# Seven block products in another order: weight sums on VectorE instead of accumulating transfers

## The chip, the cores and the metric

The program runs on one core of a Trainium2 chip. The metric is the device time of one execution in microseconds (us), as the median of several runs. The engines are TensorE (PE for matmuls, PEld for its weight loads), VectorE (DVE), ScalarE (ACT), GpSimd (POOL) and SyncE (SP). SP and POOL each issue transfers from a queue of their own, in order.

## The reference

Two layers of a decoder trunk on x (256 tokens x 2048). Each layer normalises x, projects it by one wide matrix w_in into everything that three token mixers A, B and C need and into the merge gates, runs the mixers, projects each by its own matrix, merges the three by sigmoid gates, and adds a last projection to x. The lines that matter here:

```python
h = rms_norm(x, norm_w)
proj = h @ w_in
...
y_b = (conformer_conv(ub, conv_w, conv_b, cln_w, cln_b) * jax.nn.silu(zb)) @ w_b_out
...
g = jax.nn.sigmoid(gates).reshape(b, s, N_BRANCH, D_MODEL)
merged = g[:, :, 0] * y_a + g[:, :, 1] * y_b + g[:, :, 2] * y_c
return x + merged @ w_out
```

The change touches two products per layer: the last two 512-column chunks of the gates of branch B (columns 1024 to 2047 of `g[:, :, 1]`), and two chunks of `merged @ w_out`.

## The kernel before

**Products in three parts.** Every fp32 operand is split into a high part, which a matmul takes in the fast 32-bit form, and a low rest. A product is the sum of high by high, low activation by high weight, and high activation by low weight. For the weights, ScalarE casts the raw block to `wh` (L246, `high`), and VectorE subtracts, `wl = raw - wh` (L250, `low`). These two are called the cast and the low step below. Matmuls come in the order of that sum, so the low part of the weights is needed last.

**Units.** Work on weights goes by units. An ordinary unit (`plain`) is one 512 KB block of weights, 2 x 128 rows by 512 columns: one transfer on SP's queue into a `raw` buffer (L235, four buffers), one cast, one low step (`wh` and `wl` have three buffers each), and 12 matmuls, 8 with `wh` and 4 with `wl`. `run(units, tasks)` walks a list of units. While it writes out unit n it issues the transfer of unit n+4 (after that unit's `before` functions) and the cast and the low step of unit n+2. After the products come the unit's `now` functions, one entry of `tasks`, and whatever is due of the transposes that go through memory (`zt`, `z`, `zy`).

**Order.** Inside `run` the order of VectorE is the order in which the code is written (`tc.manual_schedule(engines={nc.vector.engine})`). On the other engines a scheduler that estimates times chooses the order, TensorE's too. All queues are in order: what stands behind a waiting instruction waits too.

**Seven products.** `seven` computes a product of 2 x 2 blocks with seven block products in place of eight. It takes the first 1024 of the 2048 rows of weights and two chunks of 512 columns. The blocks of weights are B11, B12, B21, B22 (512 x 512, 1 MB each, in halves h of 512 KB); the blocks of the activations and their differences (`forms`, kept as `sums`) are prepared beforehand. Each block product is two half-units ("subs") of 6 matmuls, 4 with `wh` and 2 with `wl`, so there are 14 subs per call. They are put between ordinary units: every second unit in the w_out stretch, about every third in the gates stretch. Results gather in four PSUM banks X, Y, Z, W; V, U1, U2 and R5 are combinations that are set aside.

**Weights of the subs, before.** Two blocks are held in SBUF slots, "all" (first B11) and "two" (first B22), each fetched by two transfers on SP's queue (`fetch`, L439). The sums are made by transfers that add into the held block (`more`, L454, on POOL's queue): after the cast and the low step of a sub have read it, B12, B22 and B21 are added to "all" in turn and B12 to "two". That makes eight accumulating transfers of 512 KB per call. Only the product by B21 comes as ordinary units.

There are four such stretches, two per layer. They are called G0 and W0 (gates and w_out of the first layer) and G1 and W1 (second layer). The units of a stretch are numbered from 0 (u0, u1, ...). In W0 and W1 subs 0, 1, 2, 3 are units 2, 4, 6, 8, and units 5, 7 and 9 are ordinary; in G0 and G1 subs 0 to 3 are units 2, 4, 7 and 10.

## Time and profile before

| | |
|---|---|
| Median of 3 runs (lowest to highest) | 2014.24 us (2012.94 to 2014.68) |
| Profiled execution, its own time | 2013.33 us, span 2011.6 us |
| PE, PEld, DVE, ACT, POOL busy | 2001.1, 1677.8, 1595.5, 1093.6, 210.1 us |
| Transfers | 463.80 MB, mean 231 GB/s |
| Granted TensorE clock | 0.999 |
| Accumulating transfers L454 | 32 of 512 KB |

In the views below, a group or a timeline row names the line, the engine, the operation and the tiles written and read; `x8` is a count. In the windows view each engine has its busy time in the window and the number of its instructions; after them come the granted clock and the busy share of the transfer engines. The profile puts a matmul's end where the pipeline model has it, so rows overlap; starts are what counts.

### The profile page before, as it was taken

How to read it: one execution, taken by the hardware profiler on the slowest of the kernel's cores; microseconds unless marked ns; L12 is line 12 of the kernel's file. 1: busy time of each engine (PE TensorE's matmuls, PEld its weight loads, DVE VectorE, ACT ScalarE, POOL GpSimd, SP SyncE). 2: the span in 40 equal slices, each digit the busy share in tenths (PEclk: the TensorE clock that was granted, in tenths of full speed). 3: DMA queues.
4: the chain of work that ended last, by engine and by line, in shares of the span. 5: the costliest groups of instructions: out<-in, count | busy, mean ns of one | idle time of the engine just before them, and what ended most of it. 6: DMA issues, size and time to landing. Idle time of an engine off the chain costs nothing.

```text
span 2011.6 us, 25827 instructions
## 1 busy us (share of the span) xinstructions
PE 2001.1 (99%) x9338; PEld 1677.8 (83%) x9338; DVE 1595.5 (79%) x2124; ACT 1093.6 (54%) x1261; POOL 210.1 (10%) x316
## 2 busy tenths in 40 slices
PE   9999999999999999999999999999999999999998
PEld 8889888888888888888888988888888888888876
DVE  8667899878878876677785779988889788756777
ACT  7556555565644555455564555555656445544564
POOL 0111112100010001212210111111000100012120
PEclk9999999999999999999999999999999999999999
DMA  7788678866676678979987886788666766789795
GB/s 267 230 286 263 189 226 287 246 178 179 180 223 193 182 226 236 279 225 298 290 246 233 278 249 188 234 279 249 178 177 177 221 198 190 226 247 267 235 299 169
DMA packets 235585, 463.80 MB, mean 231 GB/s; under 512 B 17280, under 2 KB 30080, under 8 KB 235328
## 3 DMA queue, kind: packets, MB, share of 16 engines
q1 hardware_dynamic: 206592, 385.06, 62.1%
q0 software_dynamic: 27200, 73.94, 13.9%
q10 hardware_dynamic: 1664, 3.15, 0.4%
q8 instruction: 73, 1.20, 0.3%
q14 instruction: 56, 0.46, 0.1%
HBM read 429.31 MB, written 32.77 MB: 230 GB/s over the span
## 4 chain that ended last, share of the span: by engine, by line
PE 97%; DMA 2%; DVE 0%; ACT 0%; issue 0%; POOL 0%; DVEq 0%; ACTq 0%; POOLq 0%
PE acc L260 84%; PE mm L260 10%; DMA raw<-in_w_out_dram 1%; PE mm L1036 1%; DMA z<-zt 1%; PE mm L1126 0%; DMA zy<-z 0%; PE mm L1094 0%; PE mm L1231 0%; PE mm L1177 0%; ACT wh L246 0%; PE mm L795 0%; PE mm L1207 0%; PE mm L1097 0%; PE mm L1006 0%; PE mm L1236 0%
## 5 line engine op out<-in xcount | busy, mean ns | idle before, releaser
L260 PE MATMUL acc<-wh,s 128*128 128x512 f32 (+1 forms) x5088 | 1259.7, 389 | 1.4 <-ACT wh L246 1.0
L246 ACT CAST wh<-raw 128x1024 fp32r<-128x1024 f32 (+1 forms) x698 | 730.8, 1048 | 767.3 <-PE acc L260 510.8
L260 PEld LDWEIGHTS acc<-wh,s 128*128 128x128 f32 x5088 | 946.9, 188 | 190.9 <-ACT wh L246 2.4
L250 DVE TENSOR_TENSOR wl<-raw,wh 128x1024 fp32r<-128x1024 f32 (+1 forms) x699 | 846.4, 1214 | 319.6 <-ACT wh L246 317.1
L260 PE MATMUL acc<-wl,s 128*128 128x512 f32 (+1 forms) x2352 | 626.2, 388 | 0.0
L260 PEld LDWEIGHTS acc<-wl,s 128*128 128x128 f32 x2352 | 440.8, 188 | 90.2 <-DVE wl L250 1.0
L292 POOL DMA_DIRECT2D z<-zt x196 | 117.6, 616 | 1250.2 <-DVE zt L289 907.6
L605 DVE SCALAR_TENSOR_TENSOR s<-yT,cst,s 128x256 f32<-128x256 f32 x480 | 212.2, 478 | 0.0
L260 PE MATMUL mm<-wh,s 128*128 128x512 f32 x480 | 123.6, 389 | 0.1
L260 PEld LDWEIGHTS mm<-wh,s 128*128 128x128 f32 x480 | 90.0, 188 | 19.2 <-ACT wh L246 0.5
L250 DVE TENSOR_TENSOR wl<-s,wh 128x1024 fp32r<-128x1024 f32 x48 | 58.5, 1219 | 18.4 <-ACT wh L246 18.1
L246 ACT CAST wh<-s 128x1024 fp32r<-128x1024 f32 x48 | 50.5, 1053 | 40.8 <-PE acc L260 22.9
L260 PEld LDWEIGHTS mm<-s,wl 128*128 128x128 f32 x512 | 66.9, 191 | 5.0
L260 PE MATMUL mm<-wl,s 128*128 128x512 f32 x240 | 68.8, 390 | 0.0
L260 PE MATMUL mm<-s,wl 128*128 128x192 f32 x512 | 66.0, 271 | 0.0
L298 POOL DMA_DIRECT2D zy<-z x50 | 36.0, 720 | 268.7 <-DMA z<-zt 140.8
L260 PEld LDWEIGHTS mm<-wl,s 128*128 128x128 f32 x240 | 45.0, 188 | 9.7 <-DVE wl L250 0.4
L289 DVE STREAM_TRANSPOSE zt<-acc 128x512 f32<-128x512 f32 (+1 forms) x68 | 45.4, 681 | 8.2 <-PE acc L260 8.2
L454 POOL DMA_DIRECT2D s<-in_w_in_dram x16 | 19.2, 1203 | 115.7 <-DVE wl L250 100.8
L543 DVE TENSOR_TENSOR s<-zy,s 128x1024 fp32r<-128x1024 f32 x20 | 24.3, 1215 | 5.1 <-ACT s L542 5.1
L542 ACT CAST s<-zy 128x1024 fp32r<-128x1024 f32 x20 | 21.0, 1048 | 11.8 <-DVE zy L593 7.0
L1313 DVE TENSOR_TENSOR ev<-acc,ev 128x512 f32<-128x512 f32 x24 | 16.5, 688 | 11.9 <-PE acc L260 11.9
(280 smaller groups left out, 1093.4 us busy)
## 6 DMA issues: line engine op xcount, KB each, us to landing
raw<-in_w_in_dram SPq DMA_DIRECT2D x539, 512.0 KB, 4.5
raw<-in_w_out_dram SPq DMA_DIRECT2D x52, 512.0 KB, 7.2
zy<-z POOLq DMA_DIRECT2D x48, 512.0 KB, 5.2
z<-zt POOLq DMA_DIRECT2D x188, 128.0 KB, 4.6
raw<-in_w_a_dram SPq DMA_DIRECT2D x32, 512.0 KB, 3.9
raw<-in_w_c_dram SPq DMA_DIRECT2D x32, 512.0 KB, 4.4
raw<-in_w_b_dram SPq DMA_DIRECT2D x32, 512.0 KB, 5.0
s<-in_w_in_dram POOLq DMA_DIRECT2D x16, 512.0 KB, 8.3
```

Of the source, the lines that this page charges most:

```text
L246: newest_parts[0] = nc.scalar.copy(u[1], u[0])
L250: newest_parts[1] = sub = nc.vector.tensor_sub(u[2], u[0], u[1].bitcast(F32))
L260: newest[0] = nc.tensor.matmul(o, lhsT, rhs, start=start, stop=stop, skip_group_check=True)
L289: nc.vector.transpose(tmp[:, t].rearrange("p b k i -> p k b i"), src.rearrange("p k (b c) -> p k b c", b=4, c=32))
L292: nc.gpsimd.dma_start(z[:, :, :, a, :].rearrange("t b c e -> c (t b) e"), tmp[a * 32:(a + 1) * 32].rearrange("c t b k i -> c (t b) (k i)"))
L298: nc.gpsimd.dma_start(y.rearrange("p (t a) k i -> p t (a k i)", a=4), z.rearrange("t b c a e -> (b c) t (a e)"))
L454: nc.gpsimd.dma_start(grow[g][:, hs, :], block(add, h), accum_op=ALU.add)
L542: nc.scalar.copy(h, src)
L543: nc.vector.tensor_sub(l, src, h.bitcast(F32))
L605: nc.vector.scalar_tensor_tensor(o, yT[:, c, q:q + S], wq, o, op0=ALU.mult, op1=ALU.add)
L1036: nc.tensor.matmul(ps[:, q * S:(q + 1) * S], qi[i][:, hd, :], ki[j][:, 0, :], start=n == 0, stop=n == 2)
L1313: nc.vector.tensor_mul(sg[t], y[t], sg[t])
```

## The change

The seven products come in another order, with other forms of the activations where they need it, and three of the four block sums are made by VectorE. B11 and B22 are fetched at units 0 and 1 (before: 0 and 8 in the gates, 0 and 5 in w_out). B12 comes as two ordinary units, subs 2 and 3. A new hook `early` runs three units ahead, in front of the low step of the unit two ahead: for subs 2 and 3 it adds B12 to the held B11, and then B22 to the `raw` buffer that holds B12; for subs 6 and 7 it adds B22 to the held sum. Only B21 is still added by a transfer (`by_transfer`), after subs 6 and 7. B21 also comes as ordinary units, subs 10 and 11. U1 now takes two steps on VectorE, one of them after sub 3.

```diff
-        def fetch(g, b):
-            grow[g] = slot().rearrange("p (k a) t -> p k (a t)", a=2)
+        def fetch(b):
+            v = slot().rearrange("p (k a) t -> p k (a t)", a=2)
             with tc.high_priority():
                 for h in range(2):
-                    nc.sync.dma_start(grow[g][:, h * 2:h * 2 + 2, :], block(b, h))
+                    held[b, h] = v[:, h * 2:h * 2 + 2, :]
+                    nc.sync.dma_start(held[b, h], block(b, h))
+
+        def add(h, to, b):
+            nc.vector.tensor_add(held[to, h], held[to, h], held[b, h])
...
-            def more():
-                with tc.high_priority():
-                    nc.gpsimd.dma_start(grow[g][:, hs, :], block(add, h), accum_op=ALU.add)
...
-        subs = [sub(h, *v) for v in (("all", "12", act, 0, 0, X), ("21", None, act, 4, 0, X),
-                                     ("all", "22", sums, 4, 1, Z), ("two", "12", sums, 4, 0, Z),
-                                     ("all", "21", sums, 0, 0, Y), ("two", None, sums, 0, 1, Y),
-                                     ("all", None, act, 4, 1, W)) for h in range(2)]
+        subs = [sub(h, *v) for v in (("11", act, 0, 0, X), ("12", sums, 0, 1, Y), ("11", sums, 4, 1, Z),
+                                     ("11", sums, 0, 0, Y), ("22", sums, 4, 0, Z), ("21", act, 4, 0, X),
+                                     ("11", act, 4, 1, W)) for h in range(2)]
+        for h in range(2):
+            for n, last_use, b in ((2, 0, "12"), (6, 4, "22"), (12, 6, "21")):
+                if b in by_transfer:
+                    subs[last_use + h].more = lambda h=h, b=b: nc.gpsimd.dma_start(held["11", h], block(b, h), accum_op=ALU.add)
+                else:
+                    subs[n + h].early = [partial(add, h, "11", b)]
+            subs[2 + h].early = [*subs[2 + h].early, partial(add, h, "12", "22")]
         subs[1].now = [lambda: nc.scalar.copy(V, X)]
+        subs[3].now = [lambda: nc.vector.tensor_add(U1, V, Y)]
         subs[5].now = [lambda: nc.vector.tensor_sub(R5, Z, V)]
-        subs[9].now = [lambda: nc.vector.tensor_sub(U1, Y, V)]
-        subs[11].now = [lambda: nc.vector.tensor_sub(U2, V, Y)]
+        subs[7].now = [lambda: nc.vector.tensor_sub(U1, Y, U1), lambda: nc.vector.tensor_sub(U2, V, Y)]
...
+            with tc.high_priority():
+                if 0 <= n + 3 < len(units):
+                    for f in units[n + 3].early:
+                        f()
             if 0 <= n + 2 < len(units):
                 high(got[n + 2])
                 low(got[n + 2])
...
-        for n, *b in ((0, "all", "11"), (8, "two", "22")):
+        for n, b in ((0, "11"), (1, "22")):
```

How instructions stand on an engine before and after is shown at three places. In the rows, `raw`, `wh` and `wl` are a unit's buffers, `s8` a slot (a held block or a part of an activation), `long` the activation's differences before their split, `acc` the sums of ordinary units, `mm` two of the banks X, Y, Z, W.

VectorE at the start of W0, before: the split of a merged chunk (L543, from `zy`), the low steps of units 4 and 5, the first half of the split of `sums`, the low steps of units 6 and 7, the second half of that split, and the low steps of units 8 and 9.

```order
L543 TENSOR_TENSOR s8_1360_7776<-zy_1328_7619,s8_1360_7776 128x4x256
L250 TENSOR_TENSOR wl_1353_7729<-s8_1340_7707,wh_1352_7728 128x1024
L250 TENSOR_TENSOR wl_1357_7751<-raw_1355_7748,wh_1356_7750 128x1024
L543 TENSOR_TENSOR s8_1338_7703<-long_1264_7263,s8_1338_7703 128x4x256
L250 TENSOR_TENSOR wl_1363_7782<-raw_1361_7779,wh_1362_7781 128x1024
L250 TENSOR_TENSOR wl_1366_7795<-raw_1364_7792,wh_1365_7794 128x1024
L543 TENSOR_TENSOR s8_1337_7702<-long_1264_7263,s8_1337_7702 128x4x256
L250 TENSOR_TENSOR wl_1369_7815<-raw_1367_7812,wh_1368_7814 128x1024
```

The same place on VectorE after the change (its lines L443 are the adds, L555 is the split).

```order
L555 TENSOR_TENSOR s8_1363_7783<-zy_1330_7624,s8_1363_7783 128x4x256
L250 TENSOR_TENSOR wl_1356_7737<-s8_1342_7712,wh_1355_7736 128x1024
L443 TENSOR_TENSOR s8_1342_7712<-s8_1342_7712,raw_1364_7786 128x1024
L443 TENSOR_TENSOR raw_1364_7786<-raw_1364_7786,s8_1346_7719 128x1024
L250 TENSOR_TENSOR wl_1360_7758<-raw_1358_7755,wh_1359_7757 128x1024
L555 TENSOR_TENSOR s8_1340_7708<-long_1266_7269,s8_1340_7708 128x4x256
L250 TENSOR_TENSOR wl_1366_7789<-raw_1364_7786,wh_1365_7788 128x1024
L443 TENSOR_TENSOR s8_1342_7712<-s8_1342_7712,raw_1370_7820 128x1024
L443 TENSOR_TENSOR raw_1370_7820<-raw_1370_7820,s8_1346_7719 128x1024
L250 TENSOR_TENSOR wl_1369_7801<-raw_1367_7798,wh_1368_7800 128x1024
L555 TENSOR_TENSOR s8_1339_7707<-long_1266_7269,s8_1339_7707 128x4x256
L250 TENSOR_TENSOR wl_1372_7823<-raw_1370_7820,wh_1371_7822 128x1024
```

Two adds now stand in front of unit 5's low step and two more in front of unit 7's, so unit 7's low step is the tenth row where it was the sixth.

TensorE at the same place, before: units 5 to 9, each sub (`mm`) whole between ordinary units (`acc`).

```order
L260 MATMUL acc_1354_7733<-wl_1357_7751,s8_1324_7593 128x512 x4
L260 MATMUL mm_1335_7700<-wh_1362_7781,s8_1324_7593 128x512 x4
L260 MATMUL mm_1335_7700<-wl_1363_7782,s8_1324_7593 128x512 x2
L260 MATMUL acc_1354_7733<-wh_1365_7794,s8_1360_7776 128x512 x8
L260 MATMUL acc_1354_7733<-wl_1366_7795,s8_1360_7776 128x512 x4
L260 MATMUL mm_1335_7700<-wh_1368_7814,s8_1324_7593 128x512 x4
L260 MATMUL mm_1335_7700<-wl_1369_7815,s8_1324_7593 128x512 x2
L260 MATMUL acc_1354_7733<-wh_1373_7832,s8_1360_7776 128x512 x8
```

TensorE after the change; `s8_1339` is the half of `sums` that the last split on VectorE above makes.

```order
L260 MATMUL acc_1357_7740<-wl_1360_7758,s8_1326_7598 128x512 x4
L260 MATMUL mm_1338_7706<-wh_1365_7788,s8_1339_7707 128x512 x2
L260 MATMUL acc_1357_7740<-wh_1368_7800,s8_1363_7783 128x512 x8
L260 MATMUL acc_1357_7740<-wl_1369_7801,s8_1363_7783 128x512 x4
L260 MATMUL acc_1357_7740<-wh_1375_7837,s8_1363_7783 128x512
L260 MATMUL mm_1338_7706<-wh_1365_7788,s8_1339_7707 128x512 x2
L260 MATMUL mm_1338_7706<-wl_1366_7789,s8_1339_7707 128x512 x2
L260 MATMUL mm_1338_7706<-wh_1371_7822,s8_1339_7707 128x512 x4
L260 MATMUL mm_1338_7706<-wl_1372_7823,s8_1339_7707 128x512 x2
L260 MATMUL acc_1357_7740<-wh_1375_7837,s8_1363_7783 128x512 x7
```

Sub 2 now starts with two matmuls, unit 7 is put in between, and the rest of sub 2 stands behind the first matmul of unit 9. W1 has the same piece; nowhere else does TensorE's order of units change.

SP's queue at the start of W1, after the change: the final norm's weights, B11's first half, the last unit of w_b, B22's first half, w_out's units, then the second halves of both.

```order
L1416 DMA s8_2807_15956<-in_fnw_dram 128x2048
L440 DMA s8_2813_15965<-in_w_out_dram 128x2x512
L235 DMA raw_2799_15875<-in_w_b_dram 128x2x512
L440 DMA s8_2817_15972<-in_w_out_dram 128x2x512
L235 DMA raw_2814_15968<-in_w_out_dram 128x2x512
L235 DMA raw_2818_15975<-in_w_out_dram 128x2x512
L235 DMA raw_2823_15983<-in_w_out_dram 128x2x512
L235 DMA raw_2829_16008<-in_w_out_dram 128x2x512
L235 DMA raw_2835_16039<-in_w_out_dram 128x2x512
L235 DMA raw_2838_16051<-in_w_out_dram 128x2x512
L440 DMA s8_2813_15965<-in_w_out_dram 128x2x512
L440 DMA s8_2817_15972<-in_w_out_dram 128x2x512
```

Before, B22's halves stood behind the transfers of units 9 and 17, and B11's second half in front of unit 6's; now B11's second half stands behind unit 7's, and B22's first half in front of unit 0's.

## The prediction

> **What bounds the kernel now.** I read the page first, then windows, then single stretches in order of time.

> ```profile
> span 2011.6 us, 25827 instructions
> PE 2001.1 (99%) x9338; PEld 1677.8 (83%) x9338; DVE 1595.5 (79%) x2124; ACT 1093.6 (54%) x1261; POOL 210.1 (10%) x316
> PE 97%; DMA 2%; DVE 0%; ACT 0%; issue 0%; POOL 0%; DVEq 0%; ACTq 0%; POOLq 0%
> ```

> TensorE is busy for 99% of the span, and the chain that ended last runs through it for 97%. The change leaves the number of matmuls as it is. So what it can win is TensorE's waiting inside the four stretches G0, W0, G1 and W1, and what it can lose is new waiting. The windows view says how much waiting there is.

> ```profile
> core 0: us, PE busy (x) PEld busy (x) DVE busy (x) ACT busy (x) POOL busy (x), PEclk, DMA share, GB/s
> 900.00:950.00 50.00, 49.70 (x219) 40.84 (x218) 40.52 (x43) 29.21 (x32) 12.24 (x15) 1.00 0.98 299
> 1650.00:1700.00 50.00, 50.00 (x223) 41.40 (x222) 43.36 (x47) 24.07 (x25) 0.00 (x0) 1.00 0.63 189
> 1900.00:1950.00 50.00, 49.19 (x216) 40.05 (x215) 38.75 (x41) 27.44 (x30) 12.26 (x15) 1.00 1.01 314
> ```

> The window from 1650 lies outside the change and holds 223 matmuls. The start of W0 (from 900) has 219, the start of W1 (from 1900) 216, and there the transfer engines are full. Matmul starts tell more exactly; this is TensorE in W0, units 5 to 9:

> ```profile
> 931.08 1.07 PE L260 MATMUL acc<-wl,s 128*128 128x512 f32 x4
> 931.99 1.07 PE L260 MATMUL mm<-wh,s 128*128 128x512 f32 x4
> ...
> 936.97 0.61 PE L260 MATMUL mm<-wl,s 128*128 128x512 f32 x2
> 937.89 2.11 PE L260 MATMUL acc<-wh,s 128*128 128x512 f32 x8 [0.30 <-ACT wh L246]
> 939.83 1.07 PE L260 MATMUL acc<-wl,s 128*128 128x512 f32 x4
> 940.74 1.07 PE L260 MATMUL mm<-wh,s 128*128 128x512 f32 x4
> ```

> Four matmuls from 931.08 to 931.99 give 0.227 us per start. Two from 936.97 should end at 937.42, and the next starts at 937.89; the eight from there take 1.94 in place of 1.81. So one wait costs 0.60, of which 0.13 is a slow restart. Unit 9 ends at 940.74. The same in W1:

> ```profile
> 1935.70 0.61 PE L260 MATMUL mm<-wl,s 128*128 128x512 f32 x2
> 1937.05 2.14 PE L260 MATMUL acc<-wh,s 128*128 128x512 f32 x8 [0.74 <-ACT wh L246]
> 1939.03 1.08 PE L260 MATMUL acc<-wl,s 128*128 128x512 f32 x4
> 1939.94 1.07 PE L260 MATMUL mm<-wh,s 128*128 128x512 f32 x4
> 1940.85 0.61 PE L260 MATMUL mm<-wl,s 128*128 128x512 f32 x2
> 1941.54 2.11 PE L260 MATMUL mm<-wh,s 128*128 128x512 f32 x8
> 1943.49 1.08 PE L260 MATMUL mm<-wl,s 128*128 128x512 f32 x4
> ```

> By the same count 1.07 is lost ahead of 1939.03 and 0.38 around 1941.54. At the end of G1 a late transpose costs about 0.4: ScalarE, in order, waits for it and then casts late.

> ```profile
> 1858.20 1.05 ACT L542 CAST s<-zy 128x1024 fp32r<-128x1024 f32 x1 [3.71 <-DMA zy<-z]
> ```

> So 0.60 + 1.07 + 0.38 + 0.4 = 2.45 us is about all that the change can win.

> **Transfers.** Over four calls the accumulating halves fall from 32 to 8, and the ordinary halves grow by 8. That is 16 halves of 0.52 MB fewer, 8.4 of 463.8 MB. POOL's queue loses 24 of its transfers, and the `z` transposes stand behind fewer. What that is worth is read from landing times, in the full stretch 1925 to 1962, around the start of W0 (905 to 945), and in a quiet one, 750 to 790:

> ```profile
> raw<-in_w_out_dram SPq DMA_DIRECT2D x11, 512.0 KB, 10.1
> raw<-in_w_out_dram SPq DMA_DIRECT2D x13, 512.0 KB, 6.5
> raw<-in_w_in_dram SPq DMA_DIRECT2D x11, 512.0 KB, 3.7
> ```

> A block lands 10.1, 6.5 and 3.7 after its issue. I take the wait behind unit 9 in W1 as gone (-0.38; 0 if landings stay as they are) and G1's late transpose too (-0.4; 0 if it comes late for another reason). The 0.60 and 1.07 are replaced by what follows.

> **Adds.** VectorE gets 24 steps of 128x1024, and four half as long for U1. A low step has that size, so its price stands in VectorE's rows of W0:

> ```profile
> 925.18 1.18 DVE L543 TENSOR_TENSOR s<-zy,s 128x1024 fp32r<-128x1024 f32 x1
> 926.28 1.22 DVE L250 TENSOR_TENSOR wl<-s,wh 128x1024 fp32r<-128x1024 f32 x1
> 927.41 1.22 DVE L250 TENSOR_TENSOR wl<-raw,wh 128x1024 fp32r<-128x1024 f32 x1
> 928.55 1.22 DVE L543 TENSOR_TENSOR s<-long,s 128x1024 fp32r<-128x1024 f32 x1
> 929.68 2.36 DVE L250 TENSOR_TENSOR wl<-raw,wh 128x1024 fp32r<-128x1024 f32 x2
> 931.95 1.22 DVE L543 TENSOR_TENSOR s<-long,s 128x1024 fp32r<-128x1024 f32 x1
> 933.09 1.22 DVE L250 TENSOR_TENSOR wl<-raw,wh 128x1024 fp32r<-128x1024 f32 x1
> ```

> One takes 1.22, and the next starts 1.135 after it did. All of them are 24 x 1.22 = 29 us of an engine that is 79% busy, and most fit into its idle time. Here they don't: from 925.18 to 934.3 VectorE has no gap, and four adds go in.

> **W0.** The row at 927.41 is unit 5's low step. Two adds take its place. I count 1.22 around adds, since they use each other's buffers, and 1.135 elsewhere: adds at 927.41 and 928.63, unit 5's low step at 929.85 (done 931.07, and TensorE wants it at 931.08), the split at 930.98, unit 6 at 932.12, adds at 933.25 and 934.47, unit 7's low step at 935.69, done 936.9. TensorE in its new order does two matmuls of sub 2 from 931.99 and eight of unit 7, so it wants that `wl` at 931.99 + 10 x 0.227 = 934.26. It waits 2.65.

> Then it has four matmuls, to 937.8, and the first of unit 9, which needs unit 9's cast. That cast reuses unit 7's `wh` buffer, free at 936.9. Its block goes into the `raw` buffer of unit 5, so its issue follows unit 5's low step, from this row to 931.07:

> ```profile
> 928.66 0.37 SPq L235 DMA_DIRECT2D raw<-in_w_out_dram  x1
> ```

> With the landing of 6.5 it is there at 937.6, cast at 938.6: a wait of 0.8 (0.1 with a landing under 5.8, 2.3 with the 8.0 that this transfer took before, beside transfers of which two are gone). 22 more matmuls to unit 9's end (5.0) and two restarts (0.26): 943.85 in place of 940.74, **+3.1** (+1.5 to +4.5; the low end if the adds follow at 1.135 and VectorE comes to the piece earlier). Behind the adds on VectorE queue the second half of the split of `sums`, which the rest of sub 2 needs, and unit 8's low step. Both are done by 939.2, before TensorE gets there.

> **W1.** The same piece starts at 1924.67, 0.51 earlier on its axis, and unit 9's end at 1939.94, 0.80 earlier. One thing is added: B11's second half stood ahead of the three transfers of this row and now stands behind the second of them, unit 7's. Sub 1's cast needs it.

> ```profile
> 1917.49 5.10 SPq L235 DMA_DIRECT2D raw<-in_w_out_dram  x3
> ```

> ```profile
> 1921.98 1.05 ACT L246 CAST wh<-s 128x1024 fp32r<-128x1024 f32 x1
> 1925.77 1.21 DVE L250 TENSOR_TENSOR wl<-s,wh 128x1024 fp32r<-128x1024 f32 x1
> ```

> Unit 7's goes out one VectorE step after unit 6's, at about 1918.6. Issued at 1919 and landing 6 later, it is cast by 1926.1 in place of 1923.0, and sub 1's low step, at 1925.77 before, comes 0.35 late (0 to +0.9), with all behind it. In W0 unit 7's low step is done 11.72 after the piece's start (936.9 - 925.18); here it is 11.72 + 0.35 after 1924.67, at 1936.75. The rest as in W0 (0.91 + 0.8 + 5.0 + 0.26) ends at 1943.7 in place of 1939.94: +3.8. B22's first half also goes out ahead of unit 0's block, whose cast already waits:

> ```profile
> ACT wh L246 <- DMA raw<-in_w_b_dram: 2.9, 1, 2.9
> ```

> 0.52 MB at the window's 314 GB/s is 1.7 us, part of it covered by slack of unit 0: +0.4 (0 to +1.2). With -0.38 from above, W1: **+3.8** (0 to +5.5).

> **G0 and G1.** The adds for sub 2 come before unit 6's low step. In G0:

> ```profile
> 800.48 3.49 DVE L250 TENSOR_TENSOR wl<-raw,wh 128x1024 fp32r<-128x1024 f32 x3
> 812.76 1.07 PE L260 MATMUL acc<-wl,s 128*128 128x512 f32 x4
> ```

> Unit 6 is the second of these three. It ends at 805.3 in place of 802.8, and only then is its buffer free for sub 3's B12. That lands at 809.0 (3.7) to 815.4 (10.1); two adds (2.4) and unit 9's low step (1.2) follow, 812.6 to 819, and TensorE wants it at 812.76. With the accumulating transfers gone I take a landing near the quiet end and **+0.3** for each (0 to +3 each; I cut the far end, since 10.1 belongs to W1).

> **Sum.** 3.1 + 3.8 + 0.6 - 0.4 = +7.1. The profiled execution took 2013.33 (span 2011.6 and 1.7 around it), so 2020.4. The median of the runs is 0.9 above that execution: 2021.3.

> [...]

> **Rivals.** *Same:* the jam is smaller, because landings fall so far that casts and splits reach VectorE earlier and the adds start ahead of 927.41. For it: the transfer engines are full exactly there. Against it: from 925.18 on each row has a known length, and none ahead of it is removed. With 1.5 in W0, 1.5 - 0.38 in W1, nothing in G0, -0.4 in G1: +2.2, so 2016.4. *Faster:* transfers are the true limit and the adds hide. All of the 2.45 won gives 2011.8, 0.12% and still not over 0.2%; it decides only if TensorE also starts matmuls faster. The 1650 window speaks against that: it fills 50 us with 223 starts at a transfer share of 0.63. *Much slower:* sub 3's B12 lands late in G0 and G1 (the 3 us ends): +5.4 more than the sum, 2026.7. It decides from a landing of 3.9 on, and each further us there costs 2 us in total.

> [...]

> **Chances.** A difference under 0.2%, 4 us, can't be told from none. Jam as computed 0.50, much slower 0.08, same 0.38, faster 0.04. The jam's own spread is about 2018 to 2024, so nearly all of it is slower by over 0.2% (from 2018.3): slower 0.57, same 0.40, faster 0.03. Range 2015.4 (the same rival with 1 us of the jam less) to 2024.6 (upper ends of W0 and W1, and one late landing).

> **What would show it.** Right: TensorE's waits name `wl L250` in W0 and W1, unit 7's low step ends near 936.9 and 1936.8, VectorE has no gap from 925 to 939, landings behind that fall well below 10.1, and the wait at 1858 is gone. Wrong: those low steps end in time, landings stay near 10, or TensorE waits for blocks of L443 in G0 and G1.

## The result and the profile after

The changed kernel takes 2023.88 us (median of 5, 2022.65 to 2026.26), the kernel before 2014.11 on the same chip: ratio 1.0052, 95% interval 1.0038 to 1.0067. It is 9.8 us slower; 7.1 were forecast. The profiled execution, read below, is its fastest with 2022.65; the profiled one of before took 2013.33, 9.3 less.

The page of the changed kernel: span, then busy time by engine.

```profile
span 2020.9 us, 25817 instructions
PE 2005.4 (99%) x9338; PEld 1679.5 (83%) x9338; DVE 1625.4 (80%) x2152; ACT 1093.4 (54%) x1261; POOL 181.2 (9%) x292
```

VectorE has 29.9 us more work in 28 more steps, TensorE the same 9338 matmuls. Where the 9.3 us are is read by counting: the matmuls are numbered from the first, and the time between two of them is compared with the time between the same two before. Between the matmuls at 905 and 1000 us (W0) it is +2.7, between those at 1900 and 1990 (W1) +6.9; G0 is +0.04, G1 -0.06, and the rest of the program -0.2. The windows view says the same:

```profile
core 0: us, PE busy (x) PEld busy (x) DVE busy (x) ACT busy (x) POOL busy (x), PEclk, DMA share, GB/s
900.00:950.00 50.00, 47.76 (x208) 38.38 (x207) 44.76 (x49) 28.91 (x31) 6.56 (x11) 1.00 0.81 270
1900.00:1950.00 50.00, 45.97 (x184) 35.94 (x183) 40.43 (x43) 25.65 (x28) 6.11 (x10) 0.93 0.84 275
```

Matmuls fell from 219 to 208 in W0's window and from 216 to 184 in W1's, and in W1 the granted clock is 0.93. The transfer engines are less busy than before, 0.81 and 0.84.

W0, VectorE and then TensorE:

```profile
927.77 1.22 DVE L443 TENSOR_TENSOR s<-s,raw 128x1024 f32<-128x1024 f32 x1
929.02 1.22 DVE L443 TENSOR_TENSOR raw<-raw,s 128x1024 f32<-128x1024 f32 x1
...
935.96 1.22 DVE L250 TENSOR_TENSOR wl<-raw,wh 128x1024 fp32r<-128x1024 f32 x1
```

```profile
933.01 2.11 PE L260 MATMUL acc<-wh,s 128*128 128x512 f32 x8
937.23 1.19 PE L260 MATMUL acc<-wl,s 128*128 128x512 f32 x4 [2.11 <-DVE wl L250]
938.36 0.50 PE L260 MATMUL acc<-wh,s 128*128 128x512 f32 x1
```

Unit 7's low step starts at 935.96 (935.69 forecast) and TensorE, done with unit 7's eight matmuls at 934.96, waits 2.27 for it. Unit 9 follows at 938.36 with no wait of its own. W1, TensorE, and ScalarE's cast for sub 1:

```profile
1929.01 1.07 PE L260 MATMUL acc<-wl,s 128*128 128x512 f32 x4
1931.74 1.21 PE L260 MATMUL mm<-wh,s 128*128 128x512 f32 x4 [1.66 <-ACT wh L246]
1933.00 1.04 PE L260 MATMUL mm<-wl,s 128*128 128x512 f32 x2
1933.84 3.30 PE L260 MATMUL acc<-wh,s 128*128 128x512 f32 x8
1936.97 1.09 PE L260 MATMUL acc<-wl,s 128*128 128x512 f32 x4
...
1938.36 1.97 PE L260 MATMUL acc<-wh,s 128*128 128x512 f32 x8
1942.33 1.20 PE L260 MATMUL acc<-wl,s 128*128 128x512 f32 x4 [1.99 <-DVE wl L250]
1943.45 0.79 PE L260 MATMUL acc<-wh,s 128*128 128x512 f32 x1
...
1947.21 0.63 PE L260 MATMUL mm<-wl,s 128*128 128x512 f32 x2
```

```profile
1930.64 1.05 ACT L246 CAST wh<-s 128x1024 fp32r<-128x1024 f32 x1 [4.01 <-DMA s<-in_w_out_dram]
```

Two waits stand here. From 1929.01 four matmuls at 0.227 end at 1929.92, and sub 1 starts at 1931.74: 1.82 for the cast of B11's second half, which waits for its transfer. From 1938.36 eight end at 1940.17, and unit 7's low part starts at 1942.33: 2.15 for VectorE. After each wait matmuls are slow, and not only the first one, which a restart makes 0.1 longer. The eight from 1933.84 take 3.13 in place of 1.81, and the six ahead of them 2.10 in place of 1.36; nine from 1943.45 to 1947.21 take 3.76 in place of 2.04. That is 3.8 us, of which about 0.3 is restarts. The windows view, two us each, shows why:

```profile
1930.00:1932.00 2.00, 0.34 (x2) 0.26 (x2) 1.62 (x3) 1.36 (x2) 1.46 (x3) 1.00 0.99 290
1932.00:1934.00 2.00, 1.95 (x7) 1.21 (x7) 2.00 (x2) 0.63 (x1) 0.88 (x2) 0.81 0.91 332
1934.00:1936.00 2.00, 2.00 (x7) 1.52 (x6) 1.97 (x3) 1.92 (x3) 0.00 (x0) 0.50 0.75 289
1936.00:1938.00 2.00, 2.00 (x9) 1.65 (x8) 2.00 (x3) 1.50 (x2) 0.72 (x1) 0.84 0.11 17
...
1942.00:1944.00 2.00, 1.67 (x5) 1.18 (x6) 2.00 (x3) 1.34 (x2) 0.00 (x0) 0.87 0.75 271
1944.00:1946.00 2.00, 2.00 (x6) 1.56 (x5) 1.68 (x2) 0.86 (x1) 0.00 (x0) 0.50 0.75 228
1946.00:1948.00 2.00, 2.00 (x8) 1.58 (x8) 1.35 (x2) 0.78 (x2) 0.00 (x0) 0.78 0.82 222
```

TensorE is called busy in the third of them, with 7 matmuls where 9 fit at full clock and a granted clock of 0.50, called the half clock below. A row's clock is a mean, so in the first stretch the half clock lasted 0.76 + 2.00 + 0.64 = 3.4 us, up to 1936.6, and in the second 0.52 + 2.00 + 0.88 = 3.4, up to 1946.9. So W1 lost 1.82 + 2.15 + 0.5 (unit 0, late) in waits, 3.5 to the clock and 0.8 in restarts and small gaps, 8.8 in all. The kernel before lost 1.9 there in the same ways, which leaves the 6.9.

### The profile page after: what moved, and what is told of

It reads as the page before. It is cut to its first block, busy times and chain, and to the rows that moved or that the text cites. A ratio compares the mean times of both kernels' runs of the same rounds, so it can differ in the third digit from the quotient of the medians.

```text
span 2020.9 us, 25817 instructions
## 1 busy us (share of the span) xinstructions
PE 2005.4 (99%) x9338; PEld 1679.5 (83%) x9338; DVE 1625.4 (80%) x2152; ACT 1093.4 (54%) x1261; POOL 181.2 (9%) x292
## 4 chain that ended last, share of the span: by engine, by line
PE 95%; DVE 2%; DMA 2%; issue 0%; ACT 0%; DVEq 0%; SPq 0%; ACTq 0%
PE acc L260 82%; PE mm L260 10%; DVE wl L250 1%; DMA raw<-in_w_out_dram 1%; PE mm L1048 1%; PE mm L1138 0%; DMA raw<-in_w_b_dram 0%; DMA s<-in_w_out_dram 0%; DVE s L443 0%; PE mm L1106 0%; PE mm L1243 0%; PE mm L1189 0%; ACT wh L246 0%; DMA raw<-in_w_in_dram 0%; PE mm L807 0%
## 5 line engine op out<-in xcount | busy, mean ns | idle before, releaser
L260 PE MATMUL acc<-wh,s 128*128 128x512 f32 (+1 forms) x5088 | 1261.3, 389 | 0.5 <-ACT wh L246 0.3
L246 ACT CAST wh<-raw 128x1024 fp32r<-128x1024 f32 (+1 forms) x706 | 738.6, 1048 | 769.3 <-PE acc L260 506.2
L260 PEld LDWEIGHTS acc<-wh,s 128*128 128x128 f32 x5088 | 947.9, 188 | 190.9 <-ACT wh L246 2.1
L250 DVE TENSOR_TENSOR wl<-raw,wh 128x1024 fp32r<-128x1024 f32 (+1 forms) x707 | 855.8, 1213 | 309.1 <-ACT wh L246 306.6
L260 PE MATMUL acc<-wl,s 128*128 128x512 f32 (+1 forms) x2352 | 626.6, 388 | 4.3 <-DVE wl L250 4.1
L260 PEld LDWEIGHTS acc<-wl,s 128*128 128x128 f32 x2352 | 440.6, 188 | 95.7 <-DVE wl L250 6.7
L260 PE MATMUL mm<-wh,s 128*128 128x512 f32 x480 | 124.9, 392 | 1.7 <-ACT wh L246 1.7
L260 PEld LDWEIGHTS mm<-wh,s 128*128 128x128 f32 x480 | 90.9, 189 | 21.0 <-ACT wh L246 2.1
L260 PEld LDWEIGHTS mm<-s,wl 128*128 128x128 f32 x512 | 66.9, 191 | 5.0
L260 PE MATMUL mm<-wl,s 128*128 128x512 f32 x240 | 69.6, 393 | 0.0
L246 ACT CAST wh<-s 128x1024 fp32r<-128x1024 f32 x40 | 42.2, 1054 | 46.4 <-PE acc L260 18.8
L260 PE MATMUL mm<-s,wl 128*128 128x192 f32 x512 | 66.0, 271 | 0.0
L250 DVE TENSOR_TENSOR wl<-s,wh 128x1024 fp32r<-128x1024 f32 x40 | 48.8, 1220 | 11.1 <-ACT wh L246 11.0
L260 PEld LDWEIGHTS mm<-wl,s 128*128 128x128 f32 x240 | 45.1, 189 | 10.1 <-DVE wl L250 0.5
L555 DVE TENSOR_TENSOR s<-zy,s 128x1024 fp32r<-128x1024 f32 x20 | 24.3, 1213 | 1.1 <-ACT s L554 1.1
L554 ACT CAST ph<-t 128x512 fp32r<-128x512 f32 (+1 forms) x28 | 18.4, 679 | 5.4 <-PE mm L1224 5.4
## 6 DMA issues: line engine op xcount, KB each, us to landing
raw<-in_w_in_dram SPq DMA_DIRECT2D x543, 512.0 KB, 4.4
raw<-in_w_out_dram SPq DMA_DIRECT2D x56, 512.0 KB, 4.9
zy<-z POOLq DMA_DIRECT2D x48, 512.0 KB, 5.4
raw<-in_w_a_dram SPq DMA_DIRECT2D x32, 512.0 KB, 4.0
raw<-in_w_c_dram SPq DMA_DIRECT2D x32, 512.0 KB, 4.4
raw<-in_w_b_dram SPq DMA_DIRECT2D x32, 512.0 KB, 5.1
```

The lines of the kernel that those rows point to most:

```text
L246: newest_parts[0] = nc.scalar.copy(u[1], u[0])
L250: newest_parts[1] = sub = nc.vector.tensor_sub(u[2], u[0], u[1].bitcast(F32))
L260: newest[0] = nc.tensor.matmul(o, lhsT, rhs, start=start, stop=stop, skip_group_check=True)
L554: nc.scalar.copy(h, src)
L555: nc.vector.tensor_sub(l, src, h.bitcast(F32))
```

## Experiments

Theory: two losses. VectorE's row, its steps back to back at the start of W0 and W1, is too long by the four adds, and in W1 transfers come too late; the clock adds to the longer waits. Rivals: transfers decide all; the adds decide all. Medians are set against the kernel before on the same chip. W0 and W1 are the difference to before of one execution, the profiled one, counted as above.

| run | median us | ratio (95%) | W0 | W1 |
|---|---|---|---|---|
| changed kernel | 2023.88 | 1.0052 (1.0038 to 1.0067) | +2.7 | +6.9 |
| e1_b12_transfer | 2019.85 | 1.0028 (1.0018 to 1.0038) | +0.1 | +3.5 |
| e2_sp | 2021.36 | 1.0038 (1.0025 to 1.005) | +4.5 | +3.7 |
| e3_early_split | 2019.88 | 1.0029 (1.0018 to 1.0041) | +2.5 | +4.6 |
| e4_fill | 2023.06 | 1.0054 (1.004 to 1.0068) | +2.5 | +6.8 |
| f1_sp | 2020.74 | 1.0039 (1.0027 to 1.0051) | +2.4 | +3.7 |
| f2_sp_b12 | 2020.17 | 1.004 (1.0027 to 1.0053) | +3.9 | +3.2 |
| f3_sp_split | 2015.81 | 1.0014 (1.0006 to 1.0023) | +0.5 | +2.1 |
| f4_sp_b12_split | 2017.95 | 1.0028 (1.0018 to 1.0037) | +3.6 | +3.9 |
| g3_row_alone | 2020.16 | 1.0039 (1.0026 to 1.0053) | +2.4 | +3.6 |
| g1_best | 2013.57 | 1.0002 (0.9993 to 1.0011) | +0.3 | +0.9 |

**Two adds in place of four (e1).**

```diff
-        fetch, subs, extra = seven(wo, p0 * 512, mx, sums, (X, Y, Z, W), quarters(slot()), ("21",))
+        fetch, subs, extra = seven(wo, p0 * 512, mx, sums, (X, Y, Z, W), quarters(slot()), ("21", "12"))
... (the same in the gates' call)
```

> B12 is added to the held B11 by a transfer again, so VectorE has two adds in place of four at the start of each stretch. Theory (the four adds ahead of unit 7's low step are what TensorE waits for): that low step comes 2.4 us earlier, so the wait of 2.27 in W0 and of 2.15 in W1 go, and with the second one its stretch of half clock (1.6); the wait for B11's second half in W1 stays. 2023.9 - 2.3 - 2.1 - 1.6 = 2017.9 (2016.5 to 2019.5). Rival (transfers decide): 8 more accumulating transfers bring landings back towards 10 us, nothing is won, 2023 to 2026.

2019.85, just above the expected range. In W0 unit 7's low step starts 7.9 us after the row's first step in place of 10.4, and the 2.7 us are gone, with no wait over 0.15; in W1 unit 7's wait and its half clock are gone too. B11's late half keeps its wait (1.62) and a half clock. So in this execution the adds in VectorE's row are W0's whole loss, though more is transferred. The median stands above its profiled execution (2016.52), so part of this kernel's loss is in executions that left no trace.

**SP's order at the start of W1 (e2).**

```diff
-        for n, b in ((0, "11"), (1, "22")):
-            units[n].before = [*units[n].before, partial(fetch, b)]
...
+        units[0].before = [*units[0].before, partial(fetch, "11")]
+        if last:
+            first_after(units[1], 1)
+            units[2].before = [*units[2].before, lambda: fetch("22", last_dma)]
+        else:
+            units[1].before = [*units[1].before, partial(fetch, "22")]
```

`last` is the second layer, W1: there B11's second half goes out ahead of unit 1's block and B22 behind it.

> Only SP's order at the start of W1 is changed: B11's second half goes out ahead of unit 1's block, and B22 behind it, in place of ahead of unit 0's. Theory (W1's extra loss over W0's is the late second half of B11 and the half clock that follows that wait): the wait of 1.8 us ahead of sub 1 goes, with 1.7 of half clock, and 0.4 of the 0.6 ahead of unit 1; the wait for unit 7's low step stays. 2023.9 - 3.7 = 2020.2 (2019 to 2021.5). Rival (the adds alone make W1's loss, and TensorE only waits later): what is won at sub 1 is lost at unit 7, 2023 to 2025.

2021.36, in the range, but not as the theory had it. The wait for sub 1's cast and both half clocks are gone from W1, and waits for VectorE stand in their place, all three with that releaser:

```profile
1932.91 0.73 PE L262 MATMUL mm<-wl,s 128*128 128x512 f32 x2 [1.17 <-DVE wl L252]
1936.44 1.20 PE L262 MATMUL acc<-wl,s 128*128 128x512 f32 x4 [0.97 <-DVE wl L252]
1942.24 1.20 PE L262 MATMUL acc<-wl,s 128*128 128x512 f32 x4 [2.33 <-DVE wl L252]
```

The rival was half right: the late transfer hid a wait for VectorE. W0, whose code and issue times were the same, is 4.5 here: the blocks of its first units landed 9.2 to 10.1 after their issue (7.8 to 8.1 in the changed kernel's profile), so VectorE's row began 1.85 later. W0's loss is the row's length plus its start, and the start alone can move the figure of one execution by 1.8 with no change in the code.

**The splits of the sums ahead of the stretch (e3).**

```diff
-        tasks += [partial(split_at, sums, i, 4, mf[0][:, i:i + 4, :]) for i in (4, 0)]
...
         with tc.manual_schedule(engines={nc.vector.engine}):
+            for i in (4, 0):
+                split_at(sums, i, 4, mf[0][:, i:i + 4, :])
             run(units, tasks)
```

> The two splits of the sums in w_out are written ahead of the stretch in place of between its units. One of them stood ahead of unit 7's low step in the row of steps on VectorE. Theory (the length of that row is the wait): 1.135 less in W0 and in W1, and with a wait of only 1 us no half clock behind it in W1: 2023.9 - 1.1 - 1.1 - 1.6 = 2020.1 (2019 to 2022). Rival (the row isn't the limit, but the cast or the landing of unit 9 or B12 is): under 0.5 won, 2023.4 or more, since the splits then only stand elsewhere.

2019.88, in the range, for the wrong reason. The edit changed SP's order too: in W0 B11's second half now came late as in W1, and in W1 the wait for it grew to 3.6. W0 won only 0.2. This run doesn't tell the two apart; f1 and f3, where SP's order is set by hand, do.

**Filling the waits of W1 with matmuls by zero (e4).**

```diff
         for i, j in ((0, 0), (1, 0), (0, 1)):
+            if j:
+                for _ in range(pad):
+                    mult(accs[0][:, :n], zero, w_[0][:, 0, :], False, False)
...
+        if last:
+            units[3].pad, units[7].pad = 8, 10
```

> TensorE gets 18 matmuls with a block of zeros in W1 that add nothing: 8 in unit 3, ahead of the wait for sub 1's cast, and 10 in unit 7, ahead of the wait for its low step. They take 4.1 us, the time that it waits there. Theory (waiting itself brings the half clock, 3.3 us in the profile of after): the granted clock stays at 1 in W1 and the mean at 0.999, 2023.9 - 3.3 + 0.1 = 2020.7 (2019.5 to 2021.5). Rival (the half clock comes of something else, or the matmuls just lengthen the path): the clock dips as before, 2024 to 2028.

2023.06. In the profiled execution the clock stayed at 1 in W1, but W1 was 6.8 longer all the same: 4.1 are the extra matmuls, and other waits (1.1 for VectorE, 1.4 for a split) came up between them. Five executions had mean clocks of 0.996 to 0.999, and the slowest (2028.97) had the lowest. So it neither shows nor refutes that filling a wait keeps the clock.

**SP's order in both stretches, without and with the early splits, and with two adds (f1, f3, f2, f4).** Order: B11's first half, unit 0, B11's second half, units 1, 3, 5, 6, 7, then B22.

```diff
+        units[0].before = [*units[0].before, partial(fetch, "11")]
+        first_after(units[1], 1)
+        units[4].before = [*units[4].before, lambda: fetch("22", last_dma)]
```

> All adds as in the changed kernel; only SP's order is set, in W0 and W1: B11's first half, unit 0, B11's second half, units 1, 3, 5, 6, 7, then B22. So B22 isn't among the blocks that land at the start, and B11's second half goes out some 9 us earlier in W1. Theory (two separate losses: VectorE's row of four adds, and transfers that come too late in W1, with the half clock behind the longer waits): W0 keeps its 2.7, W1 falls from 6.9 to about 1.4, 2023.9 - 5.5 = 2018.4 (2017 to 2021, the upper part if the wait of 2.2 at unit 7 in W1 still brings a half clock). Rival (the late transfers only hide a wait for VectorE of the same length): W1 stays at 5 to 7, 2022 to 2024.

> SP's order as in f1_sp, four adds, and the two splits of the sums written ahead of the stretch. Theory (length of VectorE's row): 1.1 less than f1_sp in W0 and in W1 (one of the two splits stands ahead of unit 7's low step), and waits too short for a half clock: 2016.2 (2015 to 2018.5). Rival (that row isn't the limit): as f1_sp.

f1 2020.74 (expected 2018.4, up to 2021), f3 2015.81 (2016.2 expected). Their code differs in the early splits alone, two steps of 1.22 on VectorE out of the row, and their medians by 4.9 us. In the profiled executions W0 falls from +2.4 to +0.5 and W1 from +3.7 to +2.1. Two things come of it. In W0 and in W1 unit 7's low step, one split fewer ahead of it, starts 9.4 us after the row's first step in place of 10.4. And with the halves of `sums` written early, the scheduler gave TensorE another order: all six matmuls of sub 2 stand ahead of unit 7 where two did, so four more of them (0.9 us) run before unit 7's low part is wanted. What the pair shows is the price of the splits' place; the row's length is about half of it in W0. The row's length alone is shown by e1. In W1 the row began late in both runs, since unit 1's block landed behind B11's second half.

> SP's order as in f1_sp, and B12 is added to the held B11 by a transfer, so two adds in place of four. Theory: both losses are gone; W0 0 to +0.5, W1 -1 to +0.5, no wait over 1 us and no half clock: 2014.5 (2013 to 2016.5). Rival (the new order of the products or the transfers themselves cost something beside these two): 2017 or more.

> f2_sp_b12 and f3_sp_split in one. Theory: nothing is left to be waited for in W0 and W1; as f2_sp_b12 within 0.5: 2014.2 (2012.5 to 2016). A version below 2012 would need the waits of before (1.8 in W1) gone too. Rival (the splits written early delay the low steps of units 0 and 1): 1 to 3 us above f2_sp_b12.

Both wrong, 2020.17 and 2017.95 where 2014.5 and 2014.2 were expected. With two adds VectorE's row is short, but it now waits for a transfer. VectorE in W0 of f2, then landings of blocks by SP's and POOL's queue between 917 and 930:

```profile
930.94 1.21 DVE L252 TENSOR_TENSOR wl<-raw,wh 128x1024 fp32r<-128x1024 f32 x1
934.87 1.22 DVE L450 TENSOR_TENSOR raw<-raw,s 128x1024 f32<-128x1024 f32 x1 [2.71 <-DMA s<-in_w_out_dram]
```

```profile
s<-in_w_out_dram SPq DMA_DIRECT2D x2, 512.0 KB, 9.2
s<-in_w_out_dram POOLq DMA_DIRECT2D x2, 512.0 KB, 8.7
```

B22's second half landed at 934.8 here and at 931.7 in f1, where no accumulating transfers run beside it. So in these runs e1's gain and this SP order exclude each other: B22 issued late is in time only while the adds stay on VectorE.

**The row alone, and both losses taken away (g3, g1).** g3 is f1 with B11's second half back in front of unit 5's block, as in the kernel before; g1 is g3 with the early splits.

```diff
-        first_after(units[1], 1)
+        first_after(units[3], 1)
```

> g1_best without the early splits: SP's order of g1_best, the splits of the sums between the units as in the changed kernel. What is left against g1_best is VectorE's row alone. Theory: W0 +2.5 and W1 about 2 more than g1_best, with a half clock in some of the executions (waits of 2 to 2.5): 2013.6 + 2.2 + 2 = 2017.8 (2016.5 to 2020). Rival (SP's order was all of it, and the splits had only been in its way): 2013 to 2015, as g1_best.

> f3_sp_split with B11's second half one place later, in front of unit 5's block as in the kernel before, so units 1 and 3 land earlier. Theory (in W1 VectorE's row began 1.1 late in f1_sp and f3_sp_split since unit 1's block landed after B11's second half): the row begins about 1 us earlier, the waits of 1.8 and 1.1 in W1 shrink to about 1 in all, W0 stays at +0.5: 2012.9 + 0.5 + 0.8 + 0.2 = 2014.4 (2013.5 to 2015.8). Rival (B11's second half now comes late for sub 1's cast): 2016 or more, with a wait in front of sub 1.

g3 2020.16, a little above its range; g1 2013.57, just under the forecast. The two orders of TensorE, sub 2 and unit 7 in W1, first in g3 and then in g1:

```profile
1935.06 0.62 PE L262 MATMUL mm<-wh,s 128*128 128x512 f32 x2
1935.52 1.98 PE L262 MATMUL acc<-wh,s 128*128 128x512 f32 x8
1939.83 2.08 PE L262 MATMUL acc<-wl,s 128*128 128x512 f32 x4 [2.33 <-DVE wl L252]
```

```profile
1932.95 1.08 PE L262 MATMUL mm<-wh,s 128*128 128x512 f32 x4
1933.87 0.62 PE L262 MATMUL mm<-wl,s 128*128 128x512 f32 x2
1934.32 1.98 PE L262 MATMUL acc<-wh,s 128*128 128x512 f32 x8
```

Behind g3's wait the half clock came: its four matmuls from 1939.83 take 1.87 to the next start, 0.91 at full clock. g1 has none in W0 and W1; its granted clock is 1.00 from 900 to 950 and from 1900 to 1950. So more than VectorE's row parts the two runs, unlike what g3's expectation says. All that is left over 0.2 of TensorE's waits in g1 between 905 and 1965 is 0.44 in W0 and these in W1:

```profile
PE acc L262 <- DVE wl L252: 1.0, 1, 1.0
PE mm L262 <- ACT wh L248: 0.4, 1, 0.4
```

g1 keeps all 24 adds, the new order of the products and the lighter transfers, and can't be told from the kernel before. What its two changes, SP's order and the early splits, would win in the kernel before was not run. No run beat both kernels clearly; the sum of what could be won was 2.45.

**How often a wait brings the half clock (g2).** The kernel before, with added waits on TensorE.

```diff
         for i, j in ((0, 0), (1, 0), (0, 1)):
+            if j:
+                with tc.high_priority(offset=URGENT):
+                    for q in range(times):
+                        nc.scalar.copy(idle, accs[q % 2][:, q // 2 % 4 * P:][:, :P])
```

> The kernel before, with ScalarE reading a product's sums 3 to 13 times (128x128 each, about 0.25 us) in front of the low weights' matmuls of every eighth unit of 512 columns, so that TensorE waits there for 0.5 to 3.5 us. No result of this time is wanted, only how often a half clock follows a wait of each length. Theory (a fixed window in which a share of time without work counts): none after waits under 1.5 us, some after 1.6 to 2.8, nearly always after 3; each half clock lasts about 3.4 us whatever the wait was. Rival (the half clock of W1 has to do with W1): hardly any.

`times` is 3 to 13 in every eighth unit of 512 columns, else 0. There are 54 waits over 0.4 us between matmuls. A half clock, matmul starts 0.42 to 0.43 apart, is counted once, with the last wait ahead of it:

| wait, us | waits | with a half clock behind |
|---|---|---|
| 0.4 to 1.6 | 21 | 1 (0.6 long, 1.1 us behind a wait of 1.9) |
| 1.6 to 2.45 | 15 | 4 |
| 2.45 to 3.2 | 8 | 2 |
| over 3.2 | 10 | 10 |

One without (2.5 us, from 347) and one with (2.3, from 563.5), in windows:

```profile
349.00:351.00 2.00, 1.24 (x5) 1.05 (x6) 0.00 (x0) 0.70 (x2) 0.00 (x0) 1.00 0.83 275
351.00:353.00 2.00, 2.00 (x10) 1.66 (x9) 1.96 (x3) 0.66 (x2) 0.00 (x0) 1.00 0.59 226
...
567.00:569.00 2.00, 2.00 (x6) 1.53 (x6) 1.93 (x3) 0.00 (x0) 0.00 (x0) 0.54 0.00 0
569.00:571.00 2.00, 2.00 (x7) 1.56 (x6) 0.70 (x2) 0.85 (x1) 0.00 (x0) 0.60 0.77 207
```

So the half clock isn't W1's own, and the theory's three ranges came out roughly. Between 1.6 and 3.2 us the length alone doesn't decide: 6 of those 23 waits had a half clock behind them. The last section has what else was measured. In W0 and W1 of the changed kernel and the runs e1 to f4 and g3 there were 16 waits of 1.6 to 3.7 us, and seven brought it.

## Why the prediction was right, and where it was off

**W0: right.** +3.1 forecast, +2.7 measured. Unit 7's low step started 0.27 later than computed, and TensorE came a little later as well (933.01 in place of 932.45 for unit 7), so it waited 2.27 and not 2.65. The 0.8 for unit 9's block didn't come: it landed 4.1 after its issue, where 6.5 was taken. The nearness is in part luck: the same W0 code gave +4.5 in e2's profiled execution, the upper end of the range.

**W1: the mis-sized term, +3.8 against +6.9.** Two steps failed.
- The sum ran at full clock throughout. The waits of 1.82 and 2.15 in W1 each had a half clock behind them; that is 3.5 us, more than the 3.1 that W1 missed by. The range of W1 (0 to +5.5) had no room for it. Without the clock W1 stands at 3.4, near the forecast, but with its waits in other places, so that nearness is luck in part.
- B11's second half was to come 0.35 late (0 to +0.9) and TensorE not to wait for it. It waited 1.82. The transfer was put "at 1919", on times of before. It stands behind unit 7's block, which waits for unit 1's low step, and unit 1's block was late itself: B22's first half had gone out ahead of it and of unit 0's, and with B22 moved behind them, in g1 and g3, unit 1's block landed 9.1 and 7.9 after its issue in place of 11.2. Landings of the blocks of units 0, 1 and 3, in the changed kernel (issued from 1902 to 1916) and before (1900 to 1914):

```profile
raw<-in_w_out_dram SPq DMA_DIRECT2D x3, 512.0 KB, 11.2
```

```profile
raw<-in_w_out_dram SPq DMA_DIRECT2D x3, 512.0 KB, 7.7
```

B11's second half was issued at 1924.54. The whole program was 2.6 late by then, so that is 2.9 later than forecast, and unit 7's low step ended at 1942.28, again 2.9 later than its 1936.75. What was charged for B22 (+0.4 ahead of unit 0) was right, 0.5 ahead of unit 0; its price further down the queue was missed. TensorE had meanwhile waited for sub 1, so less was left to wait at unit 7, 2.15, and unit 9 had no wait.

**G0 and G1: right.** +0.3 each forecast, with 0.4 won back in G1; measured +0.04 in G0 and -0.06 in G1. In G1 sub 3's B12 landed 4.0 after its issue, and from 3.9 on it was to cost something:

```profile
1810.17 1.23 DVE L443 TENSOR_TENSOR s<-s,raw 128x1024 f32<-128x1024 f32 x1 [1.67 <-DMA raw<-in_w_in_dram]
```

TensorE lost 0.3 there, and won the late transpose's 0.4 back as forecast: the cast of `s<-zy` runs without a wait, at 1857.29.

```profile
1857.29 1.05 ACT L554 CAST s<-zy 128x1024 fp32r<-128x1024 f32 x1
```

**Landings: right, and worth little.** Blocks issued from 1927 to 1965 land after 4.8 in place of 10.1:

```profile
raw<-in_w_out_dram SPq DMA_DIRECT2D x10, 512.0 KB, 4.8
```

Of the waits shown before only 2.45 us hung on them.

**Rivals.** "Same" had the row shorter because casts come earlier; its first row stood 0.35 later than before in W0 (925.53), and in W1 2.9 later beside the 2.6 that the whole program was late by then (1930.15 against 1924.67). "Much slower" by landings in G0 and G1 didn't happen.

**The range.** Its upper end, 2024.6, is not the sum that it is said to be: the upper ends of W0 and W1 and one late landing give 2021.3 + 1.4 + 1.7 + 2.7 = 2027.1. Two of the five executions, up to 2026.26, lie above the end that was stated.

## What to carry to other kernels

VectorE, 80% busy over the program, had no gap over 0.03 us where its steps stood back to back (in W0 from 925.53 to 935.96, starts 1.11 to 1.25 apart): count the row ahead of the step that the bounding engine wants next, and look first for steps in it that could be written earlier (here two splits whose data lay ready for over 20 us; moving them won 6.6 us from g3 to g1, by a shorter row, an order of TensorE with sub 2 in one piece, and waits without a half clock behind them). B22's first half, moved to the front of SP's queue, delayed what stood behind it (unit 1's block landed 11.2 us after its issue, and 9.1 and 7.9 with B22 behind it), and what was queued behind that block's buffer (B11's second half went out 2.9 us later than forecast); follow such a chain on the new times, not on the old ones. And in g2 16 of the 33 waits of TensorE over 1.6 us had a half clock behind them, and 1 of the 21 shorter ones: price such a wait with its half clock, 1.7 us each in the changed kernel's W1 (3.41 us at a clock of 0.50).

## What the runs showed of the hardware

The half clock was not in the forecast. In the changed kernel matmuls of 512 columns started 0.427 apart behind waits of 1.82 and 2.15, at a granted clock of 0.50, and the two stretches ended 10.2 us apart. Over the whole program the five executions of the changed kernel have mean clocks of 0.996 to 0.998, the two slowest 0.996; the kernel before stays at 0.998 to 0.999.

In the changed kernel's W0 the two adds on VectorE, of which the second writes what the first reads, start 1.25 apart (927.77 and 929.02), where the other steps of 1.22 in that row start 1.13 to 1.14 apart. Two low steps in G1 start 1.26 apart (1804.88 and 1806.14), so the cause stays open.
